# The tiles of one SBUF pool made a little longer, so that the pools behind it begin elsewhere

## The chip, the core and the metric

The kernel runs on one core of a Trainium2 chip. Times are device microseconds (us) of one execution, from launch to end. Rows of the profile come from one profiled execution; the times named as runs were taken without it.

## What is computed

One layer of a streaming encoder on x of 1024 tokens by 1024 features, in float32:

```
h  = rms_norm(x, norm1_g);  u = h @ w_in
A  = silu(layer_norm(causal depthwise conv(31) of (a * sigmoid(gate))))   # 512 wide
B  = rms_norm(chunkwise retention(rotary q, rotary k, v)) * silu(g)       # 4 heads of 128
x  = x + concat([A, B]) @ w_out
h  = rms_norm(x, norm2_g)
x  = x + square(relu(h @ w_ff1)) @ w_ff2        # 1024 -> 4096 -> 1024
out = rms_norm(x, final_g)
```

## The kernel before

**Every large product is three matmuls.** Each operand is split into a high and a low part (type fp32r). The helper `mm3` (lines 136, 137, 138 of the profile) issues, for a stationary pair lh, ll and a moving pair rh, rl: lh with rh, lh with rl, ll with rh. A matmul has 128 stationary columns and 512 moving columns. The order in which the profile names the operands is by name and not by role.

**Stages in the order of TensorE's program.** The input projections, the convolution's gate, the rotary products and the retention (0 to about 308 us from the span's start); the output projection `out_proj`, first for the retention half (`wo`, 8 blocks of 128 tokens), then for the convolution half (`woa`, 8 blocks), 24 matmuls of 512 columns a block and projection (about 308 to 430 us); one plain pair of feed-forward columns, `plain_pair(0)` (430 to 455); fifteen Strassen pairs, `strassen_pair(p)`, each of seven products M1, M2, M6, M5, M7, M3, M4 of 12 matmuls, 84 in all (454 to 755); the second feed-forward product, `ff2_group` (755 to 1046); the last rows, the final norm and the stores (to the end). The order on each engine comes from a scheduler, and the engines wait for each other by semaphores.

**Pools.** SBUF tiles come from pools, each with a number of slots of one size; a slot is as long as the longest tile that shares it, rounded up to 32 bytes. The pools that matter, in the order of their addresses, with the byte at which the first slot begins in each partition:

| pool | slots, bytes a slot | first byte | place within 256 bytes | what lies in it |
|---|---|---|---|---|
| wp | 13 of 8192 | 51264 | 64 in every slot | `cols`, `w`, `h2`, `t`, `bf`: split weights and columns |
| rawp | 2 of 4096 | 157760 | 64 | loads |
| cp | 7 of 4224 | 165952 | 64, 192, 64, 192, ... | `xt`, `glu`, `y`, `xn`, `w1h`, `w1l`, `t12`, `t34`, `ysum` |
| sp | 11 of 2048 | 195520 | 192 in every slot | `mh`, `ml`, `a22`, `hid`, `part` and others |
| hx | 1 of 8192 | 220096 | 192 | `tx` |

The slot of cp is 4224 bytes long because of `glu`, 1054 numbers of 4 bytes (4216); all other tiles there have 4096 bytes or less. 4224 is 16.5 times 256. Slices that `mm3` takes begin at multiples of 512 bytes within a tile.

**Who is stationary and who moves.** In `out_proj` the stationary tiles are `mh`, `ml` (sp) and the moving ones `w` (wp). In a Strassen pair the stationary tiles are `w1h`, `w1l` (cp) and, in M4, `a22` (sp); the moving ones are `h2` and `t` (wp), and in M7 `t` as the high and `tx` (hx) as the low part. In the other stages both operands lie in wp. The seven slots of cp are taken in turn, so that `w1h` and `w1l` of a product lie now at 64, now at 192. `ident` and `ones`, operands of the 128-column matmuls and transposes, lie at 128 in an earlier pool.

**Three places in which TensorE waits for others.** In the `woa` stage a block's second half of 12 matmuls is followed by an addition (L632), a sum of squares, a power and `xn` (L608), and the transposes `pt` of that `xn` (L617) stand in TensorE's program behind the next block's first half. Ahead of the Strassen pairs the columns of `h2` go to DRAM and come back (`bf`), and VectorE and ScalarE make the sums `t`, `tx` from them. At the end of the last pair, loads of `w2raw` and `xr` start `ff2_group`.

Of the kernel before, what the change touches and what calls it, by code (L numbers as in the profile page):

```python
# [8 lines left out]
F32 = mybir.dt.float32  # L9
# [6 lines left out]
P = 128  # L16
D = 1024
S = 1024
# [3 lines left out]
PAD = KT - 1  # L22
# [8 lines left out]
GB = 2  # L31
NG = NB // GB
WARM = 11
QUOTA = (4, 16, 11, 11, 13, 33, 22, 14)
NPAIR = NF // 2

# [2 lines left out]
def hybrid_layer_kernel(  # L39
# [20 lines left out]
    cp = pool("cp", 7)  # L60
# [206 lines left out]
    glu, marks = [], []  # L267

    def glu_gate(accs):
        g = cp.tile([P, PAD + S], F32, tag="c", name="glu")  # L270
        nc.gpsimd.memset(g[:, 0:PAD], 0.0)
        for h in range(2):
            zg = sp.tile([P, HALF], F32, tag="s", name="zg")
            nc.vector.tensor_tensor(zg, accs[1][h], r1_row[h], ALU.mult)
            sg = sp.tile([P, HALF], F32, tag="s", name="sg")
            nc.scalar.activation(sg, zg, AF.Sigmoid)
            sr = sp.tile([P, HALF], F32, tag="s", name="sr")
            nc.gpsimd.tensor_tensor(sr, sg, r1_row[h], ALU.mult)
            nc.vector.tensor_tensor(g[:, PAD + h * HALF : PAD + (h + 1) * HALF], accs[0][h], sr, ALU.mult)
        glu.append(g)  # L280
        marks.append(len(pe_log))
# [17 lines left out]
    with tc.manual_schedule(engines=ordered):  # L299

        idle = pr.tile([P, 4, P], F32, tag="r", name="idle")
        for i in range(WARM):
            nc.tensor.matmul(idle[:, i % 4], lhsT=ones, rhs=ones, start=True, stop=True)
# [30 lines left out]
    nc.sync.dma_start(trg, trig)  # L334

    glu_gate(first)
    wv = chunk_w(0)
    for q in range(2):
        accs[q].append(bank(1))
    for d in range(ND):  # L340
        glu_proj(w, 1, accs, d, 1)
    glu_gate(accs)

    def glu_tile(w, j):
# [14 lines left out]
    for j in range(2):  # L359
        if j == 1:  # L360
            wk = chunk_w(3)
        glu_gate(glu_tile(w, j))
# [213 lines left out]
    i = 0  # L576
    for (a, b), n in zip(zip(marks, marks[1:]), QUOTA):
        for j in range(n):
# [441 lines left out]
```

## Time and profile before

| | |
|---|---|
| runs, median of 3 | 1077.8 us (1075.88 to 1078.59) |
| the profiled execution | 1076.53 us |
| its span, first to last instruction | 1074.8 us |
| TensorE matmul busy (page) | 1039.7 us, 97%, 4772 instructions |
| VectorE busy | 803.4 us, 75% |
| ScalarE busy | 381.5 us, 35% |
| mean granted TensorE clock | 0.991 of full speed |

Busy time of TensorE is a union of overlapping matmuls: one lasts longer than the time until the next begins. What a stream of matmuls costs is therefore read from the starts.

### The profile page before, as it was taken

The numbers are of one execution on the slowest core, as the hardware profiler recorded it, in microseconds if no ns is written. First come the engines' busy times: TensorE is split into PE (matmuls) and PEld (weight loads), VectorE is DVE, ScalarE is ACT, GpSimd is POOL, SyncE is SP. The second block draws the span as 40 slices with busy tenths as digits, with TensorE's granted clock in tenths as the row PEclk, the third lists the DMA queues.
The fourth block names the chain that finished last, engine by engine and source line by source line (L and its number), as shares of the span: only waits on it lengthen the run. The fifth ranks groups of instructions, "written<-read, shape, count | busy, mean of one in ns | idle before, by whom it ended". The sixth has DMA issues, their size and how long they took to land.

```text
span 1074.8 us, 12628 instructions
## 1 busy us (share of the span) xinstructions
PE 1039.7 (97%) x4772; PEld 856.7 (80%) x4772; DVE 803.4 (75%) x975; ACT 381.5 (35%) x601; POOL 69.4 (6%) x134
## 2 busy tenths in 40 slices
PE   9999999999999989969999999999999999999996
PEld 7888888888888777748888888887788888888885
DVE  5397769999796455687677676776998878777857
ACT  7511111144531465333232332322453333433423
POOL 0400110021000311000000000000000000000003
PEclk9999999999999999979999999999999999999998
DMA  9412011002241024615334444356546344253324
GB/s 357 166 40 79 26 53 59 21 14 66 92 140 63 1 59 155 219 68 176 138 135 169 138 161 138 133 185 213 199 143 250 117 176 164 95 186 103 92 78 156
DMA packets 55020, 134.88 MB, mean 126 GB/s; under 512 B 5424, under 2 KB 13744, under 8 KB 54576
## 3 DMA queue, kind: packets, MB, share of 16 engines
q1 hardware_dynamic: 54960, 134.09, 36.4%
q8 instruction: 37, 0.61, 0.2%
q14 instruction: 23, 0.19, 0.1%
HBM read 97.11 MB, written 36.96 MB: 125 GB/s over the span
## 4 chain that ended last, share of the span: by engine, by line
PE 52%; DVE 2%; DMA 1%; issue 1%; POOL 1%; ACT 0%; SPq 0%; POOLq 0%; DVEq 0%; ACTq 0%
PE acc L136 9%; PE acc L138 9%; PE acc L137 9%; PE pa L138 5%; PE pa L137 5%; PE pa L136 5%; PE pb L138 4%; PE pb L137 4%; PE pb L136 4%; DMA xr<-x1M 1%; DVE ot L917 0%; DMA w2raw<-in_w_dram 0%; DVE blk L909 0%; ACT trash L936 0%; POOL var L938 0%
## 5 line engine op out<-in xcount | busy, mean ns | idle before, releaser
L136 PE MATMUL acc<-w 128*128 128x512 f32 x454 | 176.8, 389 | 0.8 <-ACT w L187 0.8
L137 PE MATMUL acc<-w 128*128 128x512 f32 x454 | 176.2, 388 | 0.0
L138 PE MATMUL acc<-w 128*128 128x512 f32 x454 | 175.9, 388 | 0.0
L373 DVE SCALAR_TENSOR_TENSOR y<-glu,vec,y 128x1024 f32<-128x1024 f32 x120 | 153.7, 1290 | 2.0
L136 PEld LDWEIGHTS acc<-w 128*128 128x128 f32 x454 | 85.2, 188 | 19.8 <-ACT w L187 1.3
L136 PE MATMUL acc<-w,cols 128*128 128x512 f32 x256 | 100.1, 391 | 0.0
L137 PE MATMUL acc<-w,cols 128*128 128x512 f32 x256 | 99.8, 390 | 0.0
L138 PE MATMUL acc<-w,cols 128*128 128x512 f32 x256 | 99.8, 390 | 0.0
L137 PEld LDWEIGHTS acc<-w 128*128 128x128 f32 x454 | 85.2, 188 | 17.6
L138 PEld LDWEIGHTS acc<-w 128*128 128x128 f32 x454 | 85.2, 188 | 17.6
L187 ACT ACTIVATE w<-xr 128x1024 fp32r<-128x1024 f32 (+1 forms) x56 | 56.2, 1004 | 105.5 <-PE acc L138 57.4
L188 DVE TENSOR_TENSOR w<-xr,w 128x1024 fp32r<-128x1024 f32 (+1 forms) x56 | 64.7, 1155 | 27.9 <-ACT w L187 27.8
L889 DVE TENSOR_TENSOR blk<-acc,blk 128x512 f32<-128x512 f32 x112 | 72.7, 686 | 11.8 <-PE acc L138 11.6
L113 ACT ACTIVATE w<-raw 128x1024 fp32r<-128x1024 f32 (+1 forms) x36 | 34.8, 966 | 96.9 <-PE acc L138 71.6
L136 PE MATMUL pa<-t,w1h 128*128 128x512 f32 x120 | 47.9, 399 | 10.0 <-ACT part L751 10.0
L138 PEld LDWEIGHTS acc<-w,cols 128*128 128x128 f32 x256 | 48.1, 188 | 9.8
L137 PEld LDWEIGHTS acc<-w,cols 128*128 128x128 f32 x256 | 48.1, 188 | 9.8
L136 PEld LDWEIGHTS acc<-w,cols 128*128 128x128 f32 x256 | 48.1, 188 | 9.8
L136 PE MATMUL acc<-w,mh 128*128 128x512 f32 x128 | 52.0, 406 | 0.0
L187 ACT ACTIVATE w1h<-t 128x1024 fp32r<-128x1024 f32 x30 | 31.7, 1057 | 55.9 <-PE pb L138 55.9
L136 PE MATMUL acc<-cols,w 128*128 128x512 f32 x128 | 50.0, 392 | 1.1 <-ACT w L113 0.9
L137 PE MATMUL acc<-w,mh 128*128 128x512 f32 x128 | 50.7, 396 | 0.0
(193 smaller groups left out, 2094.6 us busy)
## 6 DMA issues: line engine op xcount, KB each, us to landing
raw<-in_w_dram SPq DMA_DIRECT2D x34, 512.0 KB, 3.6
w2raw<-in_w_dram SPq DMA_DIRECT2D x30, 512.0 KB, 4.5
raw<-in_w_in_dram SPq DMA_DIRECT2D x23, 512.0 KB, 3.3
xt<-in_x_dram SPq DMA_DIRECT2D x8, 512.0 KB, 9.0
raw<-in_w_out_dram SPq DMA_DIRECT2D x8, 512.0 KB, 3.3
xr<-in_x_dram SPq DMA_DIRECT2D x16, 256.0 KB, 3.0
stash<-full SPq DMA_DIRECT2D x16, 256.0 KB, 2.6
out_dram<-ot SPq DMA_DIRECT2D x16, 256.0 KB, 2.0
```

Source lines behind the costliest of these rows:

```text
L113: nc.scalar.activation(w[:, 0, i], raw[:, i], AF.Copy)
L136: nc.tensor.matmul(acc, lhsT=lh, rhs=rh, start=first, stop=False, **kw)
L137: nc.tensor.matmul(acc, lhsT=lh, rhs=rl, start=False, stop=False, **kw)
L138: pe_log.append(nc.tensor.matmul(acc, lhsT=ll, rhs=rh, start=False, stop=last, **kw))
L187: nc.scalar.activation(hi, src, AF.Copy)
L188: nc.vector.tensor_tensor(lo, src, hi.bitcast(F32), ALU.subtract)
L373: nc.vector.scalar_tensor_tensor(y, glu[c][:, k : k + S], tap(k), y, ALU.mult, ALU.add)
L889: nc.vector.tensor_tensor(t, acc[lane][r], t, ALU.add)
```

## The change

One tile of cp gets longer: 1024 + 64 numbers, 4352 bytes, 17 times 256. Nothing reads or writes the 34 numbers that are added at its end. Every slot of cp grows with it, from 4224 to 4352 bytes, and what lies behind cp moves up by 896 bytes.

```diff
@@ -31,6 +31,7 @@
 GB = 2
 NG = NB // GB
 WARM = 11
+ALIGN = 256
 QUOTA = (4, 16, 11, 11, 13, 33, 22, 14)
 NPAIR = NF // 2
 
@@ -267,7 +268,7 @@
     glu, marks = [], []
 
     def glu_gate(accs):
-        g = cp.tile([P, PAD + S], F32, tag="c", name="glu")
+        g = cp.tile([P, S + ALIGN // 4], F32, tag="c", name="glu")
         nc.gpsimd.memset(g[:, 0:PAD], 0.0)
         for h in range(2):
             zg = sp.tile([P, HALF], F32, tag="s", name="zg")
```

The instructions, their order on each of the five engines and their waits are the same in both programs; addresses alone differ. After the change the slots of cp begin at 165952 + 4352 i, sp at 196416 and hx at 220992: 64 within 256 bytes for each of them. `ident` and `ones` stay at 128. Line numbers are one higher behind the new constant.

## Rows read from the trace of the kernel before

**Rows 1.** The page, part 1: busy us, share of the span, instructions of TensorE.

```profile
PE 1039.7 (97%) x4772; PEld 856.7 (80%) x4772; DVE 803.4 (75%) x975; ACT 381.5 (35%) x601; POOL 69.4 (6%) x134
```

**Rows 2.** Stretches: length, busy us (instructions) of PE, PEld, DVE, ACT, POOL; clock; DMA share; GB/s.

```profile
300.00:400.00 100.00, 94.44 (x466) 76.42 (x465) 63.87 (x86) 39.68 (x75) 15.28 (x40) 1.00 0.20 64
...
458.00:472.00 14.00, 4.66 (x11) 3.23 (x12) 14.00 (x13) 6.26 (x6) 0.00 (x0) 0.51 0.12 37
...
500.00:600.00 100.00, 100.00 (x435) 81.42 (x434) 72.62 (x99) 30.60 (x42) 0.00 (x0) 1.00 0.42 145
...
900.00:1000.00 100.00, 100.00 (x442) 82.56 (x441) 77.34 (x89) 35.72 (x40) 0.00 (x0) 1.00 0.37 121
```

**Rows 3.** Groups by line and form: count | busy us, mean ns of one | idle before.

```profile
L137 PE MATMUL acc<-w 128*128 128x512 f32 x450 | 175.1, 389 | 0.0
...
L188 DVE TENSOR_TENSOR w<-xr,w 128x1024 fp32r<-128x1024 f32 x49 | 59.8, 1221 | 20.3 <-ACT w L187 20.1
...
L188 DVE TENSOR_TENSOR w1l<-t,w1h 128x1024 fp32r<-128x1024 f32 x30 | 36.5, 1221 | 15.7 <-PE pb L137 15.7
```

**Rows 4.** Groups of PE, 508.3 to 510.9 us: a product with `w1h`, `w1l` at 64.

```profile
L137 PE MATMUL pa<-t,w1h 128*128 128x512 f32 x4 | 1.6, 389 | 0.0
```

**Rows 5.** Groups of PE, 605.35 to 608.0 us: a product with `w1h`, `w1l` at 192.

```profile
L137 PE MATMUL pa<-t,w1h 128*128 128x512 f32 x4 | 1.6, 393 | 0.0
```

**Rows 6.** Groups of PE, 474.99 to 477.6 us: M7 with `w1h`, `w1l` at 64.

```profile
L137 PE MATMUL pa<-tx,w1h 128*128 128x512 f32 x4 | 1.6, 395 | 0.0
L136 PE MATMUL pa<-t,w1h 128*128 128x512 f32 x4 | 1.6, 389 | 0.0
```

**Rows 7.** Groups of PE, 572.0 to 574.6 us: M7 with `w1h`, `w1l` at 192.

```profile
L136 PE MATMUL pa<-t,w1h 128*128 128x512 f32 x4 | 1.6, 393 | 0.0
...
L137 PE MATMUL pa<-tx,w1h 128*128 128x512 f32 x4 | 1.6, 388 | 0.0
```

**Rows 8.** Timeline of PE: start us, us, line, matmul; ends of three series of matmuls.

```profile
346.21 0.39 PE L138 MATMUL acc<-w,ml 128*128 128x512 f32 x1
...
351.09 0.39 PE L138 MATMUL acc<-w,ml 128*128 128x512 f32 x1
...
482.97 0.40 PE L136 MATMUL pa<-h,w1h 128*128 128x512 f32 x1
...
508.01 0.39 PE L136 MATMUL pa<-t,w1h 128*128 128x512 f32 x1
...
513.45 0.39 PE L136 MATMUL pa<-t,w1h 128*128 128x512 f32 x1
...
735.40 0.40 PE L136 MATMUL pa<-h,w1h 128*128 128x512 f32 x1
```

**Rows 9.** Timeline, all engines, a block of the `woa` stage; in brackets the idle time before.

```profile
373.33 1.06 PE L617 MATMUL pt<-ident,xn 128*128 128x128 f32 x8 [1.18 <-DVE xn L608]
...
377.23 0.69 DVE L632 TENSOR_TENSOR blk<-acc,blk 128x512 f32<-128x512 f32 x1 [0.71 <-PE acc L138]
...
382.02 1.06 PE L617 MATMUL pt<-ident,xn 128*128 128x128 f32 x8 [1.18 <-DVE xn L608]
```

**Rows 10.** Timeline of PE and DVE between the plain pair and the Strassen pairs.

```profile
430.46 1.07 PE L617 MATMUL pt<-ident,xn 128*128 128x128 f32 x8 [0.28 <-DVE xn L608]
...
446.65 2.29 DVE L188 TENSOR_TENSOR t<-bf,t 128x2048 fp32r<-128x2048 f32 x1 [1.38 <-ACT t L187]
...
465.05 0.80 PE L136 MATMUL pa<-t,w1h 128*128 128x512 f32 x1 [10.01 <-ACT part L751]
```

**Rows 11.** The chain that ended last: start us, us, what; two stretches.

```profile
470.21 0.43 PE pa L138
...
743.08 5.07 DMA w2raw<-in_w_dram
...
755.32 5.39 DMA xr<-x1M
```

**Rows 12.** Timeline of PE, where the second feed-forward product waits.

```profile
761.84 0.50 PE L136 MATMUL acc<-w 128*128 128x512 f32 x1 [0.84 <-ACT w L187]
```

## Prediction

> **What bounds the kernel now.** I read the page's busy times first. TensorE has matmuls in flight for 97% of the span, and no other engine reaches 80% [rows 1]. That share alone says little, since matmuls overlap; the stretches and the starts say whether TensorE streams or waits. From 500 to 600 us and from 900 to 1000 it is busy without a gap at full clock, while VectorE has a quarter of its time free [rows 2]. Yet the same 100 us hold 435 matmuls in the Strassen pairs and 442 in the second feed-forward product. All are 128 by 128 by 512. So a Strassen matmul costs more, and neither a wait nor the clock accounts for it. That difference is what this change can touch.
>
> **How large it is, from starts.** Two Strassen products with every operand at place 64 run from 508.01 to 513.45 us: 24 matmuls in 5.44 us, 226.7 ns each. In `out_proj`, where the stationary tile lies at 192 and the moving one at 64, 21 matmuls run from 346.21 to 351.09, 232.4 ns each. Thirteen whole pairs, with `w1h` and `w1l` sometimes at 64 and sometimes at 192, run from 482.97 to 735.40: 252.43 us for 13 x 84 matmuls, 231.2 ns each [rows 8].
>
> **Whether the place is the cause.** The duration of one matmul follows the spacing (389 ns where starts are 226.7 apart), and groups give it to the nanosecond. Line 137 sends the low moving part past the high stationary part. With both at 64 it takes 389 [rows 4]; with the stationary tiles at 192 it takes 393 [rows 5]. That alone could be something about 192. M7 separates the two, because `tx` itself lies at 192. With the stationary tiles at 64, line 137 takes 395 and line 136, whose operands share a place, 389 [rows 6]. With the stationary tiles at 192 the order turns round: line 137 takes 388, and line 136 takes 393 [rows 7]. The fast matmul is therefore the one whose operands begin at one place, whichever that is. The change gives every 512-column matmul that.
>
> VectorE doesn't show any such thing: the subtraction of 1024 columns takes 1221 ns where all tiles lie at 64 and 1221 ns over the 30 whose places are mixed [rows 3]. So I cost the other engines at nothing: same instructions, same order, same durations.
>
> A rule that speaks against the change: by the Trainium skill (page TensorE: Matmul & The Clock Gate, section Step-by-step: what each phase is for) the engine has two independent SBUF read ports, one for the moving operand and one for loading weights, and loading the next weights takes nothing from the running matmul. By that rule places would not matter and the sum would be nothing instead of 7 us. Rows 6 and 7 disagree by 5 to 7 ns a matmul.
>
> **The change part by part.** Nothing is added, removed or moved in any queue. Each term is a number of matmuls times the difference between what they cost now and 226.7 ns, less what disappears in a wait.
>
> *Retention half of `out_proj`.* 8 blocks x 24 = 192 matmuls at 232.4, so 192 x 5.7 ns = 1.1 us. TensorE is not held up here by another engine for long, so this shows in full.
>
> *Convolution half of `out_proj`.* Also 192 matmuls, but half of them are covered. The additions behind a second half start at 377.23, released by TensorE; `pt` starts at 382.02, 4.8 us later, and TensorE has by then been idle for 1.18 us. In between lie transposes and the next block's first 12 matmuls [rows 9]. Shorten these twelve and the wait grows by as much. The second half lies on the path. That leaves 8 x 12 matmuls and the very first half: 108 x 5.7 = 0.6 us. The other 0.5 us is hidden.
>
> *Plain pair.* Its 74 or so mixed matmuls run ahead of the 10.01 us wait that ends at 465.05. From 446.65 VectorE works through the sums and splits of the columns almost without a pause, and between 458 and 472 it is busy for 14.00 of 14.00 us [rows 2, 10]. That work begins from `pt` at 430.46 by way of DRAM. So the end of the wait moves with `pt`, by the 1.7 us above, and the plain pair's 0.4 us only lengthens the wait.
>
> *Strassen pairs.* An aligned pair would last 84 x 226.7 ns = 19.04 us; the thirteen last 252.43 / 13 = 19.42. 13 x 0.38 = 4.9 us. The first pair, from the return of the clock to 482.97, has some 48 matmuls at full clock: 0.2 us. Of the last pair only what runs before about 741 us counts, 24 matmuls, 0.1 to 0.2 us. Then a chain of two loads with VectorE between them (743.08, and 755.32) sets when the next stage starts at 761.84, and the 0.84 us wait there takes up the rest, some 0.3 us [rows 11, 12]. Together 5.2 us.
>
> *The second feed-forward product and everything before 308 us.* Both operands lie at 64 already, 389 ns [rows 3]: nothing.
>
> Sum: 1.1 + 0.6 + 5.2 = 6.9, say 7.0 us. The profiled execution took 1076.53, so 1069.5 for it. It was 1.3 us faster than the median of the runs; against that median the forecast is 1077.8 - 7.0 = **1070.8 us**.
>
> **What no row shows, bounded from both sides.** The first is the spacing of `mh` and `a22` once they lie at 64. Nearest below is 226.7, the aligned products. Nearest above is 231.2, the mean of the pairs now, and then nothing is gained. I take 226.7, because cp already holds aligned tiles and gives that. The second is the clock after the long wait. It is at half, 0.51 in that stretch [rows 2], and stays there when matmuls resume; starts are then 0.43 us apart [rows 11]. About nine matmuls pay 0.20 us each. The wait moves and gets 0.4 us longer, so that the return may come earlier, for up to 1.8 us less, or later, for as much more. I take no change. Third, whether place costs anything at half clock: nine matmuls by 0 to 6 ns, nothing to count.
>
> **The rivals.**
>
> *No change, 1077.8.* The spacing goes with the stage and not with the place: in the Strassen pairs and `out_proj` tiles from cp and sp are also freshly written by ScalarE and VectorE while TensorE reads. For it: all the slow groups stand in those stages. Against it: rows 4 to 7 come from one stage with the same writers, and the slow line turns with the place. The page SBUF — State Buffer of the Trainium skill (section SBUF: two separate sides) says that TensorE never waits on another engine's port; it too gives no change. Chance 0.08.
>
> *Gain swallowed, about 1076 to 1074.* The matmuls get faster and another engine becomes the bound in the Strassen pairs. Then 1.7 us from `out_proj` stay and some of the 5.2. VectorE has 72.62 us of work in 100 [rows 2]; a pair at 19.04 us raises that to 74, not to 100. A bound would have to come from latency between a product and its copy, where no idle time of TensorE shows. Chance 0.09.
>
> *Slower.* The granted clock falls where it did not before. The place is the `woa` stage. There TensorE waits 1.18 us a block and the clock stays at 1.00 all the same [rows 2, 9]; each wait grows by 0.07. At half clock a matmul costs 0.20 us more. The 7.0 us are gone after 35 such matmuls, and the run is slower by 0.3% (3.2 us, about what a measurement of this kernel can tell from no change) after 51, two blocks' worth. A wait of 1.25 instead of 1.18 us hardly does that. Chance 0.03; about 1085 if three blocks fall: 72 x 0.20 = 14.4, less 7.0, is 7.4 slower.
>
> **How the numbers follow.** The forecast has the remaining 0.80. Its own range is 7.0 less or more by the clock's 1.8 and by the runs' scatter of 1 us: 1068.0 to 1073.5. The range reaches up to 1075.0, which takes in the loss of four fifths of the Strassen gain; unchanged and slower lie outside. Faster by over 0.3%: 0.80 and half of the swallowed case, 0.85. Within 0.3%: the other half and no change, 0.12. Slower 0.03.
>
> **What would show it.** Every group of 512-column matmuls in `out_proj` and the Strassen pairs at 388 to 390 ns, M7's line 137 (then 138) among them, except beside a transpose or a wait. Thirteen pairs in 247.5 us. 442 matmuls between 500 and 600 us, as now between 900 and 1000. The waits ahead of `pt` at about 1.25 us, the long wait at about 10.4, the wait ahead of the second feed-forward product at 1.0 to 1.2. VectorE's 1221 ns unchanged. The forecast is wrong if aligned groups stay at 393 or more, if a new idle time of TensorE stands in the pairs, or if the clock is at half anywhere but after the long wait, at the start and at the end.

## The result, and the profile after

The runs after have a median of 1070.88 us (1070.27 to 1071.17, four runs), those of before in the same comparison 1078.12 us (1075.88 to 1078.59, four runs). The ratio is 0.9936 with a 95% interval of 0.9919 to 0.9953: 7.2 us less, of which the interval allows 5.1 to 8.7. The forecast was 1070.8.

The profiled execution after took 1070.78 us, with a span of 1069.0 us and a mean granted clock of 0.991. That is 5.75 us less than the profiled execution before. The sections below take this pair of traces apart.

The page of the kernel after, part 1, answers to [rows 1]:

```profile
PE 1033.0 (97%) x4772; PEld 856.1 (80%) x4772; DVE 802.4 (75%) x975; ACT 381.5 (36%) x601; POOL 69.4 (6%) x134
```

TensorE alone has changed, by 6.7 us of busy time; the other engines keep theirs to about 1 us. The stretches of the same trace answer to [rows 2], with the same columns:

```profile
458.00:472.00 14.00, 5.14 (x12) 3.61 (x13) 14.00 (x13) 5.78 (x6) 0.00 (x0) 0.51 0.11 37
300.00:400.00 100.00, 94.15 (x471) 77.09 (x470) 63.90 (x87) 40.37 (x77) 15.29 (x40) 1.00 0.19 64
500.00:600.00 100.00, 100.00 (x443) 82.81 (x442) 74.15 (x103) 31.84 (x45) 0.00 (x0) 1.00 0.42 148
900.00:1000.00 100.00, 100.00 (x442) 82.56 (x441) 78.21 (x92) 35.71 (x39) 0.00 (x0) 1.00 0.35 119
```

Between 500 and 600 us there are now 443 matmuls where there were 435, one more than the 442 of the second feed-forward product. The stage is still busy without a gap: more matmuls fit because each takes less. VectorE's share there rises only to 74.15.

The groups by line of the kernel after (lines are one higher; columns as in [rows 3]):

```profile
L138 PE MATMUL acc<-w 128*128 128x512 f32 x450 | 175.1, 389 | 0.0
...
L137 PE MATMUL acc<-w,mh 128*128 128x512 f32 x128 | 51.6, 403 | 0.0
L139 PE MATMUL acc<-w,ml 128*128 128x512 f32 x128 | 50.3, 393 | 0.0
L138 PE MATMUL acc<-w,mh 128*128 128x512 f32 x128 | 50.2, 392 | 0.0
...
L138 PE MATMUL pb<-h,w1h 128*128 128x512 f32 x120 | 46.7, 389 | 0.0
L139 PE MATMUL pb<-h,w1l 128*128 128x512 f32 x120 | 46.7, 389 | 0.0
```

These Strassen groups stand at 389 ns, the duration that only aligned products had. Three groups of `pa<-t` (lines 137, 138 and 139) stand at 398, 402 and 396, because they also hold the first matmuls behind the long wait, at half clock. The groups of `out_proj` fall too, but stop at 392, 393 and 403. That is a sign of something that the forecast had not counted.

### The profile page after: what moved, and what is told of

The parts are those of the page before. It is cut to its first block, busy times and chain, and to the rows that moved or that the text cites. A ratio compares the mean times of both kernels' runs of the same rounds, so it can differ in the third digit from the quotient of the medians.

```text
span 1069.0 us, 12628 instructions
## 1 busy us (share of the span) xinstructions
PE 1033.0 (97%) x4772; PEld 856.1 (80%) x4772; DVE 802.4 (75%) x975; ACT 381.5 (36%) x601; POOL 69.4 (6%) x134
## 4 chain that ended last, share of the span: by engine, by line
PE 52%; DMA 1%; DVE 1%; POOL 1%; ACT 1%; issue 1%; SPq 0%; POOLq 0%; ACTq 0%; DVEq 0%
PE acc L137 9%; PE acc L138 9%; PE acc L139 9%; PE pa L139 5%; PE pa L137 5%; PE pa L138 5%; PE pb L139 4%; PE pb L138 4%; PE pb L137 4%; DMA w2raw<-in_w_dram 1%; DVE ot L918 0%; DMA xr<-x1M 0%; DVE blk L910 0%; ACT trash L937 0%; POOL var L939 0%
## 5 line engine op out<-in xcount | busy, mean ns | idle before, releaser
L137 PE MATMUL acc<-w,mh 128*128 128x512 f32 x128 | 51.6, 403 | 0.0
L139 PE MATMUL acc<-w,ml 128*128 128x512 f32 x128 | 50.3, 393 | 0.0
```

The lines of the kernel that those rows point to most:

```text
L137: nc.tensor.matmul(acc, lhsT=lh, rhs=rh, start=first, stop=False, **kw)
L139: pe_log.append(nc.tensor.matmul(acc, lhsT=ll, rhs=rh, start=False, stop=last, **kw))
```

## Where the microseconds lie in the two traces

The table pairs starts of the same instruction in the two programs. The timeline of TensorE after has these rows for the later column; the ones of before are in [rows 8, 9, 10, 12].

```profile
372.67 1.06 PE L618 MATMUL pt<-ident,xn 128*128 128x128 f32 x8 [1.23 <-DVE xn L609]
...
381.32 1.06 PE L618 MATMUL pt<-ident,xn 128*128 128x128 f32 x8 [1.23 <-DVE xn L609]
...
429.66 1.06 PE L618 MATMUL pt<-ident,xn 128*128 128x128 f32 x8 [0.40 <-DVE xn L609]
...
464.57 0.79 PE L137 MATMUL pa<-t,w1h 128*128 128x512 f32 x1 [10.80 <-ACT part L752]
...
482.65 0.39 PE L137 MATMUL pa<-h,w1h 128*128 128x512 f32 x1
...
730.17 0.39 PE L137 MATMUL pa<-h,w1h 128*128 128x512 f32 x1
...
755.28 0.39 PE L139 MATMUL acc<-w 128*128 128x512 f32 x1
755.79 0.50 PE L137 MATMUL acc<-w 128*128 128x512 f32 x1
```

| place | before | after | earlier by | forecast |
|---|---|---|---|---|
| first `pt` of the `woa` stage | 373.33 | 372.67 | 0.7 | 1.2 |
| last `pt` | 430.46 | 429.66 | 0.8 | 1.7 |
| end of the long wait | 465.05 | 464.57 | 0.5 | 1.7 |
| second Strassen pair begins | 482.97 | 482.65 | 0.3 | 1.9 |
| fifteenth Strassen pair begins | 735.40 | 730.17 | 5.2 | 6.8 |
| second feed-forward product, behind its wait | 761.84 | 755.79 | 6.1 | 6.9 |
| end of the span | 1074.8 | 1069.0 | 5.8 | 7.0 |

Thirteen pairs took 730.17 - 482.65 = 247.52 us, the 247.5 that the forecast named, and 19.04 us each. This term is 252.43 - 247.52 = 4.9 us, as forecast. `out_proj` gave 0.8 us instead of 1.7. The long wait gave 0.3 us of that back: the load of `bf` from DRAM was issued 0.9 us earlier but released VectorE only 0.3 us earlier. From the fifteenth pair to the matmul of the second feed-forward product that waits [rows 12], another 0.8 us is gained, where the prediction counts 0.1 to 0.2. The idle time ahead of that matmul is 0.12 us now (from 755.28 + 0.39 to 755.79); it was 0.84, and 1.0 to 1.2 had been named. In the profiles of three kernels below that also have everything at one place (the first, the one with `ident` moved, and the last) it is 0.91, 0.88 and 0.60 us, and the matmul starts between 755.8 and 756.0 us in all of them. What moves the loads ahead of it was not looked into. Behind that matmul 0.3 us is lost again, and no cause is shown for it.

## The experiments

Every kernel below starts from the changed kernel. The work and its order stay the same, and what lies where is all that is edited. Each was also timed against the kernel before on the chip that it ran on. Line numbers shift with the lines that an edit adds: the second matmul of `mm3` is line 137 before, 138 after, and 139 where a pad adds one line.

**Is it the same place, or the place 64?** A pad of 128 bytes ahead of all pools puts every large operand at 192.

```diff
+    pad = const.tile([P, 32], F32, name="pad")
     ones = const.tile([P, P], F32, name="ones")
```

> A pad of 128 bytes ahead of all pools: every operand of the 512-column matmuls lies at 192 instead of 64, all still at one place; ident and ones at 0. Theory (equality of places counts): all groups stay at 388 to 390 ns, time 1070.9 us within 1.5. Rival (the place 192 itself is slow, or 64 fast): about 4160 matmuls lose 5.7 ns each, 23.7 us, so about 1094.6 us, and groups in the projections rise to 393 to 397 ns.

Measured: 1071.4 us against 1077.15 before on that chip, ratio 0.9946 (0.9927 to 0.9965). Two groups of its profile:

```profile
L139 PE MATMUL acc<-w 128*128 128x512 f32 x450 | 175.1, 389 | 0.0
...
L138 PE MATMUL pb<-h,w1h 128*128 128x512 f32 x120 | 46.7, 389 | 0.0
```

With all at 192 nothing is slower. The rival, by which 192 is a slow place, would have shown 1094.6 us.

**Is it the distance, or the slots of cp?** The changed kernel's slots are a multiple of 256 long, which might matter by itself. Here they keep that length, and a pad behind rawp moves cp, sp and hx to 192 while wp stays at 64.

```diff
+    pad = pool("pad", 1).tile([P, 32], F32, name="pad")
     cp = pool("cp", 7)
```

> After, with a pad of 128 bytes between rawp and cp: all slots of cp, sp and hx at 192, wp at 64. Slots of cp are still 17 times 256 bytes long. Theory (equality of places): every matmul of the Strassen pairs and of the output projection is mixed; a pair costs 84 x 232 = 19.5 instead of 19.04 us, 14.5 pairs 6.6 us, the output projection 0.9 us, so about 1078.4 us, as slow as before or a little slower. Rival (it is the change from slot to slot within cp that costs, or the length of a slot): the Strassen pairs stay at 19.04 us and only the output projection loses its 0.9, so about 1071.8 us.

Measured: 1078.88 us against 1077.15, ratio 1.0011 (1.0001 to 1.002). The gain is gone. The stretch from 500 to 600 us, and the first matmuls of the second and of the fifteenth pair in its timeline:

```profile
500.00:600.00 100.00, 100.00 (x433) 81.15 (x432) 71.73 (x98) 30.45 (x41) 0.00 (x0) 1.00 0.42 147
```

```profile
483.76 0.39 PE L138 MATMUL pa<-h,w1h 128*128 128x512 f32 x1
...
737.09 0.39 PE L138 MATMUL pa<-h,w1h 128*128 128x512 f32 x1
```

433 matmuls instead of 443, and 253.33 us for thirteen pairs, 19.49 each. The change's new slot length is there and does nothing without the common place.

**Half of the change.** Slots of cp as before, sp and hx moved to 64 by a pad.

```diff
-        g = cp.tile([P, S + ALIGN // 4], F32, tag="c", name="glu")
+        g = cp.tile([P, PAD + S], F32, tag="c", name="glu")
+    pad = pool("pad", 1).tile([P, 32], F32, name="pad")
     sp = pool("sp", 11)
```

> Half of the change: slots of cp as before (4224 bytes, 64 and 192 in turn), but a pad of 128 bytes ahead of sp, so that sp and hx begin at 64. Theory: the output projection keeps its whole gain (0.9 us in the profiles), M4 of the fifteen pairs is aligned (180 matmuls x 5.7 = 1.0 us), M7 gains where its weights lie at 64 (some 0.3 us); the rest, w1h and w1l at 192, stays slow. So 2.2 us less than before, about 1075.9 us. Rival (cp alone matters): 1078.1 us, with mh at 396 ns as before.

Measured: 1076.47 us against 1077.15, ratio 0.9988 (0.9977 to 1.0): 0 to 2.5 us faster, less than a measurement can tell from no change, and it holds the 2.2 us. The groups tell more:

```profile
L139 PE MATMUL acc<-w,mh 128*128 128x512 f32 x128 | 50.2, 392 | 0.0
...
L139 PE MATMUL pb<-h,w1h 128*128 128x512 f32 x120 | 47.2, 393 | 0.0
...
L139 PE MATMUL pa<-t,a 128*128 128x512 f32 x60 | 23.4, 389 | 0.0
```

`out_proj` is at 392 as after the whole change, M4 at 389, and products with `w1h` are at 393 as before. Each pool moves the groups whose stationary tile it holds.

**Why `out_proj` stops at 392.** In the changed kernel two windows of one block of the retention half, behind its transposes and later on, give these groups (group, count | busy, mean ns | idle):

```profile
L137 PE MATMUL acc<-w,mh 128*128 128x512 f32 x2 | 0.8, 395 | 0.0
L139 PE MATMUL acc<-w,ml 128*128 128x512 f32 x2 | 0.8, 394 | 0.0
```

```profile
L138 PE MATMUL acc<-w,mh 128*128 128x512 f32 x5 | 1.9, 389 | 0.0
L139 PE MATMUL acc<-w,ml 128*128 128x512 f32 x4 | 1.6, 389 | 0.0
```

The first matmuls behind a group of 128-column transposes are still slow; later the series settles at 389. `ident`, which the transposes read, lay at 128. So it and `ones` were moved to 64 by allocating `vec` and two small tiles ahead of them.

```diff
+    NV = vecs.shape[1]
+    vec = const.tile([P, NV], F32, name="vec")
+    mhalf = const.tile([P, H], F32, name="mhalf")
+    eps1 = const.tile([P, 1], F32, name="eps1")
     ones = const.tile([P, P], F32, name="ones")
...
     ident = const.tile([P, P], F32, name="ident")
...
-    mhalf = const.tile([P, H], F32, name="mhalf")
...
-    eps1 = const.tile([P, 1], F32, name="eps1")
...
-    NV = vecs.shape[1]
-    vec = const.tile([P, NV], F32, name="vec")
```

> After, with vec, mhalf and eps1 allocated ahead of ones and ident, so that these two lie at 64 as well; nothing else moves. In the profile after, the first 5 to 9 matmuls behind each group of transposes still take 231 to 236 ns. Theory (the transposes' operand at 128 leaves them out of step): they settle at once, L137 of acc<-w,mh falls from 403 towards 398 and the output projection gains up to 0.8 us more, so about 1070.1 us. Rival (the transposes themselves do it, wherever ident lies): the same as after, 1070.9 us, and the first matmuls behind transposes as slow as there.

Measured: 1071.15 us against 1077.15, ratio 0.9948 (0.9927 to 0.9969), as the changed kernel. Its groups:

```profile
L137 PE MATMUL acc<-w,mh 128*128 128x512 f32 x128 | 51.6, 403 | 0.0
...
L138 PE MATMUL acc<-w,mh 128*128 128x512 f32 x128 | 50.2, 392 | 0.0
```

My theory on `ident` falls: 403 and 392 as before the move. The place of `ident` is not what leaves the series out of step. Nor does it take a transpose. In the changed kernel, M4 of the last pair starts behind a pause of 0.36 us, with all its operands at 64 and no 128-column matmul near it:

```profile
747.01 0.50 PE L137 MATMUL pa<-t,a 128*128 128x512 f32 x1 [0.36 <-DVE part L756]
747.35 0.39 PE L138 MATMUL pa<-t,a 128*128 128x512 f32 x1
...
748.96 0.39 PE L139 MATMUL pa<-t,a 128*128 128x512 f32 x1
...
751.68 0.39 PE L139 MATMUL acc<-w 128*128 128x512 f32 x1
```

From 747.35 to 748.96 the starts are 230.0 ns apart on the mean (seven spacings), and from there to 751.68 they are 226.7 apart (twelve). So a break in the series is enough. Whether the 128 columns of the transposes or their unsplit type add to it was not tried.

**How does the cost go with the distance?** The pad of the second experiment with 32, 64 and 96 bytes.

> After, with a pad of 32 bytes between rawp and cp: cp, sp and hx at 96, wp at 64, so stationary and moving operands of the Strassen pairs and the output projection begin 32 bytes apart within 256. With 128 bytes apart a pair took 19.49 us, with none 19.04. Theory (only the same place is fast): 19.4 to 19.5 us a pair, time about 1078.5 us. First rival (the cost grows with the distance): a quarter of it, 19.15 us a pair, about 1072.8 us. Second rival (32 bytes still count as one place): 19.04 us, about 1071.2 us.

> The same with 64 bytes: 128 against 64. Theory (only the same place is fast): 19.4 to 19.5 us a pair, about 1078.5 us. First rival (grows with the distance): half, 19.27 us, about 1075 us. Second rival (64 bytes are one place): 19.04 us, about 1071.2 us.

> The same with 96 bytes: 160 against 64. Theory: 19.4 to 19.5 us a pair, about 1078.5 us. First rival: three quarters, 19.38 us, about 1077 us. Second rival: 19.04 us only if places are counted coarser than 96 bytes, about 1071.2 us.

Measured against 1077.03 us of before on their chip: 1079.9 (ratio 1.0026, 1.0016 to 1.0036), 1079.89 (1.0024, 1.0015 to 1.0033) and 1081.02 us (1.0029, 1.0018 to 1.004). The stretch from 500 to 600 us in the three profiles, in that order:

```profile
500.00:600.00 100.00, 100.00 (x430) 80.53 (x429) 70.54 (x97) 29.42 (x41) 0.00 (x0) 1.00 0.42 147
```

```profile
500.00:600.00 100.00, 100.00 (x431) 80.57 (x430) 70.80 (x97) 30.34 (x41) 0.00 (x0) 1.00 0.43 147
```

```profile
500.00:600.00 100.00, 100.00 (x429) 80.46 (x428) 70.23 (x97) 29.55 (x41) 0.00 (x0) 1.00 0.43 147
```

With 32 bytes thirteen pairs run from 485.02 to 739.73, with 96 from 484.48 to 739.96; each start is its row in the timelines:

```profile
485.02 0.40 PE L138 MATMUL pa<-h,w1h 128*128 128x512 f32 x1
...
739.73 0.40 PE L138 MATMUL pa<-h,w1h 128*128 128x512 f32 x1
```

```profile
484.48 0.39 PE L138 MATMUL pa<-h,w1h 128*128 128x512 f32 x1
...
739.96 0.40 PE L138 MATMUL pa<-h,w1h 128*128 128x512 f32 x1
```

That is 19.59 and 19.65 us a pair; with 64 they run from 484.05 to 738.77, 19.59 each. Both rivals fall: the cost does not grow with the distance from nothing, and 32 bytes apart is not one place. My own 19.4 to 19.5 was a little low. Every distance tried costs 0.45 to 0.61 us a pair, and 128, the one that occurs in the kernel before, is the cheapest of them.

**Is there a better place than 64?** Operands at 64 begin within a block of 256 bytes. This kernel has 64 bytes fewer ahead of the large pools and so puts all of them at 0.

```diff
-    mhalf = const.tile([P, H], F32, name="mhalf")
+    halves = const.tile([P, H + 1], F32, name="halves")
+    mhalf, eps1 = halves[:, 0:H], halves[:, H : H + 1]
...
-    eps1 = const.tile([P, 1], F32, name="eps1")
...
-        r1[t] = const.tile([P, 1], F32, name=f"r1_{t}")
+        if t != 1:
+            r1[t] = const.tile([P, 1 + (t == 0)], F32, name=f"r1_{t}")
+            if t == 0:
+                r1[0], r1[1] = r1[0][:, 0:1], r1[0][:, 1:2]
```

> After, with 64 bytes fewer ahead of the large pools (mhalf and eps1 in one tile, the first two r1 in one tile): every operand of the 512-column matmuls begins at a multiple of 256. Theory (places need only be the same): 226.7 ns a matmul and 1071 us, as with 64 and with 192. Rival (64 and 192 are both off a line of memory, and its start is faster): 512 columns at 2.4 GHz are 213.3 ns, so up to 13 ns a matmul less over some 4200 matmuls, down to 1016 us at most, and groups below 389 ns.

Measured: 1070.54 us against 1077.03, ratio 0.9934 (0.9919 to 0.9949), the changed kernel's time. Its stretch:

```profile
500.00:600.00 100.00, 100.00 (x443) 82.84 (x442) 74.14 (x102) 32.17 (x44) 0.00 (x0) 1.00 0.41 146
```

0, 64 and 192 give the same 443 matmuls. So the rival falls: what 226.7 ns has over its 213.3 ns is the same at all three places, and its cause stays open.

## Why the prediction was right, step by step

*The cause.* Matmuls are fast when all their operands begin at one place within 256 bytes, whichever place that is: shown by three common places (0, 64 and 192: 1070.5, 1070.9 and 1071.4 us) and by four distances that are slow. The inversion of `tx` [rows 6, 7] had said so before any run. The second experiment alone shows it too: the same instructions, with cp, sp and hx moved by 128 bytes, lose the whole gain. That the count is by 256 bytes and not by 512 shows in cp: after the change its slots lie at 64 and 320 within 512 in turn, and its groups stand at 389.

One sentence of the prediction is too narrow: "The fast matmul is therefore the one whose operands begin at one place". The weights of the next matmul count as well. A product of the kernel before, from 546.9 to 549.7 us, has `w1h` at 64, `w1l` at 192 and the moving tiles at 64:

```profile
L138 PE MATMUL pa<-t,w1l 128*128 128x512 f32 x4 | 1.6, 397 | 0.0
L137 PE MATMUL pa<-t,w1h 128*128 128x512 f32 x4 | 1.6, 396 | 0.0
L136 PE MATMUL pa<-t,w1h 128*128 128x512 f32 x4 | 1.6, 389 | 0.0
```

Line 136 has its own weights and those of the next matmul at 64. Line 137 has its own at 64 too, but the next ones, `w1l`, lie at 192, and it is slow. Line 138 has its own at 192 and the next ones at 64, and is slow as well. That is not an echo of the slow line 137 ahead of it: in the window of [rows 6] line 138 stands behind a slow line 137 and takes 388. After the change all these places agree, so the forecast did not suffer from it; one for tiles of which only some agree would have.

By the Trainium skill (page TensorE: Matmul & The Clock Gate, section Step-by-step: what each phase is for) weights and moving data are read through two independent ports, and loading the next weights takes nothing from the running matmul. These rows do not agree: line 137 takes 389 with the next weights at 64 [rows 4] and 396 with them at 192.

*Strassen pairs.* Forecast 4.9 us for thirteen, measured 4.9.

*`out_proj`.* Mechanism right, size too large. The step that failed is "192 at 232.4, so 192 x 5.7 ns" and the like for the other half, which took every matmul to 226.7. It measured 0.7 us up to the first `pt` and 0.1 us from there to the last, where its terms give 1.2 and 0.5, because the first matmuls behind each group of transposes stay slow. Over the 340 spacings of `out_proj` with no transpose in between, read from the starts in the two traces, the mean fell from 232.6 to 228.6 ns and not to 226.7. A half of 12 with transposes ahead of it spends much of its length in these first matmuls.

*Hidden savings.* Right in the `woa` stage: the wait ahead of the first four `pt` went from 1.18 to 1.23 us, where 1.25 was named. For the long wait nothing is shown: 10.4 us was named, and it is 10.80 us here but 9.98, 9.98 and 10.04 in the three other kernels with everything at one place, so that it differs between executions by more than the 0.4 us in question. The wait ahead of the second feed-forward product was missed: it shrank to 0.12 us where 1.0 to 1.2 was named, and the term for the last pair, 0.1 to 0.2 us, measured 0.8.

*The clock.* Right. It was at 0.51 between 458 and 472 us in both traces. TensorE resumed 0.5 us earlier and did one matmul more at half clock, so that the gain at the second pair was 0.3 us.

*The rivals.* "No change" fell with the groups at 389, "swallowed" with a stretch that has 443 matmuls and no idle time, "slower" with a clock of 1.00 between 300 and 400 us. One sign that the prediction named against itself did appear, once in fifteen pairs: M4 of the last pair waits 0.36 us for VectorE (0.1 before). It costs nothing that shows: the last kernel of the experiments has no such wait, and there the second feed-forward product starts no earlier, at 756.04 us.

*Luck.* The total came out nearer than its parts. The sum stood at 7.0 us; the profiled pair moved by 5.75, with 0.9 us missing in `out_proj`, 0.7 lost between the last `pt` and the second pair, 0.7 gained beyond the forecast behind the fifteenth pair, and 0.3 lost after that. The runs moved by 7.2 us, but the four runs of before spread over 2.7 us. On the two chips of the experiments before has medians of 1077.15 us (20 runs) and 1077.03 us (22 runs), and the three kernels with everything at one place stand 5.8, 6.0 and 6.5 us below it there. The forecast less what `out_proj` fell short of it, 6.1 us, lies among these; that the first comparison gave the full 7.0 is luck, as far as these runs tell.

## What to carry to other kernels

In a stream of matmuls that TensorE bounds, compare the number of matmuls per 100 us between stages: where it differs without idle time or a lower clock, look at where the stationary and the moving tiles begin within 256 bytes. A pool's slot takes the length of its longest tile, so one odd tile moves every pool behind it; lengthening it to a multiple of 256 cost 128 bytes a slot here, and helps only if the pools also begin at one place, as the second experiment shows. Don't move a single pool without working out its distance from the others: with 32 to 96 bytes between them the runs were 0.2 to 0.3% slower than before the change.

## What the runs showed of the hardware that was not expected

The cost depends on whether places agree and hardly on how far they differ: 19.04 us a pair at no distance, 19.59 at 32 bytes, 19.65 at 96 and 19.49 at 128. A series also has to settle: behind 128-column transposes aligned matmuls begin at 394 to 395 ns and come down to 389 within the same block, moving `ident` did not change that (403 for the first line of `mm3` in both kernels), and a pause of 0.36 us without any transpose does the same. And both meetings of a moving operand count, that with the matmul's own weights and that with the next ones: one alone made 397 and 396 ns of 389. Why the places have to agree, no run here shows.
